# A hybrid decoder step: order of the opening, the new tokens' values, and the sums of the conv norm

## The chip, the core and the metric

The kernel runs on one core of a Trainium2 chip. The metric is the device time of one execution in microseconds, the median of three runs. Lower is better.

## What is computed

One layer of a decoder with two branches, on 512 prompt tokens and 32 new tokens (8 sequences of 4) together, 544 columns in all. Everything is f32.

```
h = RMSNorm_pre(x); z = h @ w_in        # columns: q | k | v | gate_attn | conv_a | conv_b | gate_conv
attention, 12 heads x 128: three dilated windows (128,1), (512,4), (2048,16), T5 bias, merged by softmax weight
conv, 512 channels: u = a * sigmoid(b); depthwise causal conv, width 31; LayerNorm over channels; swish; pointwise
mix = [att * silu(gate_attn), conv * silu(gate_conv)]
y = x + RMSNorm_post(mix @ w_out)
outputs: y for prompt and new tokens, new conv state, new k/v rows, the k/v cache shifted by 4 rows
```

The RMSNorm in front is not applied to x. Its per-token factor 1/rms (`R`) multiplies the products afterwards, since it is one number per token.

## The kernel before

**Projection.** `w_in` is cut into 60 blocks of 128 columns, `w_out` into four of 512. An f32 product is made as three products in a faster number format: x and the weights are split into a high and a low part (`xh`, `xl`, `wh`, `wl`), and TensorE adds xh·wh, xl·wh and xh·wl. One column block takes 96 products x 2 halves of 272 tokens. ScalarE casts `wh`, POOL subtracts to get `wl` (lines 819, 820); a piece of four 128x128 tiles is called a split.

**Opening.** `project_first` makes the first three column blocks side by side, by pieces of x as they land. Meanwhile `square` (line 283, ScalarE) sums the squares of five blocks of tokens (`mix` for four blocks of 128 tokens, `xt` for the 32 new ones), `token_rsqrt` makes the root on ScalarE (line 204) and a correction step on VectorE (lines 205 to 210), builds five diagonal matrices (line 212, `diagx`), and TensorE spreads them over all partitions by products with ones (`rbx`). ScalarE copies the two results to `R`. Only with `R` can the three column blocks be taken out of their banks.

**Side work.** After each half of a projection `tick` advances generators: attention of one head of the prompt, the new tokens' attention (`samples`, three groups of four heads), and the conv. In `v_phase` of the new tokens a unit is one sequence: eight pieces of four matmuls with a tile position each, seven over the cached rows (`kvf`, `kvm`) and one over the 32 new rows (`vtm`). The four sequences of a half stand side by side in one bank; `gather` copies it (`osb`, line 719), TensorE transposes it (`ot`), and VectorE writes the parts out.

**Conv norm.** `conv_ln` sums four channel blocks `cc` with ones on TensorE: `pm` for the mean, `pvar` over the squares `csq`, each in two halves of 272 tokens, f32 products that TensorE makes in several passes.

**Order.** All engines run their instructions in the order in which the program is written (`in_order`); a wait holds whatever is behind it on the same engine. All but one of the transfers are issued by SyncE in that order too. The copy of the cache (`bulk`) is spread over the run: at each tick it is issued up to START + PACE bytes per column that TensorE has been given (`pe`).

Of the kernel before, what the change touches and what calls it, by code (L numbers as in the profile page):

```python
# [42 lines left out]

UTK, UTV = 3.75, 3.3

START, PACE = 4_000_000, 166.3

NF = 3

# [36 lines left out]
def body(tc, xT, xtok, gpost, w_in, w_out, ckv, cconv, relb, vecs, pww, c_oht, c_ohr, c_lmr, c_tm, c_pick,  # L86
# [191 lines left out]
    def load_xtok(b):  # L278
        dma(xt_of(b), xtok[b * P:min(b * P + P, TOK)])

    def square(b):
        t_ = xt_of(b)
        nc.scalar.activation(t_, t_, AF.Square, accum_out=sumsq[:P if b < 4 else NS, b:b + 1])
# [182 lines left out]
    def conv_ln():  # L466
        cc = mixg[3]
        def load_pw(n):
            pw = apool.tile([P, 4, P], F32, tag="pw", name=f"pw{n}")
            dma(pw, pww[:, :, n * P:(n + 1) * P])  # L470
            return pw

        pw = load_pw(1)

        for hf in range(2):
            sl = slice(hf * HT, hf * HT + HT)
            pm = bank("z", f"pm{hf}")
            for ct in range(4):
                mm(pm[:, :HT], ones, cc[:, ct, sl], start=(ct == 0), stop=(ct == 3))
            for ct in range(4):  # L480
                nc.vector.scalar_tensor_tensor(cc[:, ct, sl], pm[:, :HT], -4.0, cc[:, ct, sl], op0=ALU.mult,
                                               op1=ALU.add)
            yield
        ri = apool.tile([P, TOK], F32, tag="q", name="cri")
        for hf in range(2):
            sl = slice(hf * HT, hf * HT + HT)
            csq = [apool.tile([P, 2, HT], F32, tag="up", name=f"csq{hf}_{i}", bufs=2) for i in range(2)]
            for ct in range(4):
                nc.scalar.activation(csq[ct // 2][:, ct % 2, :], cc[:, ct, sl], AF.Square)
            yield  # L490
            pv = bank("z", f"pvar{hf}")
            for ct in range(4):
                mm(pv[:, :HT], ones, csq[ct // 2][:, ct % 2, :], start=(ct == 0), stop=(ct == 3))
            vs = apool.tile([P, HT], F32, tag="ccv", name=f"vs{hf}")
            nc.scalar.copy(vs, pv[:, :HT])
            yield
            yield from rsqrt(ri[:, sl], vs, HT, 4.0, apool, tag="up")
            yield
        for ct in range(4):
            nc.vector.tensor_tensor(cc[:, ct, :], cc[:, ct, :], ri, op=ALU.mult)  # L500
            nc.scalar.activation(cc[:, ct, :], cc[:, ct, :], AF.Identity, bias=V(V_LNB, ct), scale=V(V_LNG, ct))
            th = apool.tile([P, TOK], F32, tag="up", name=f"cth{ct}", bufs=2)
            nc.scalar.activation(th, cc[:, ct, :], AF.Tanh, scale=0.5)
            nc.vector.scalar_tensor_tensor(cc[:, ct, :], th, 1.0, cc[:, ct, :], op0=ALU.add, op1=ALU.mult)
            yield

        res = [cc[:, 0, :]] + [apool.tile([P, TOK], F32, tag="up", name=f"pwo{i}", bufs=2) for i in range(2)]
        res.append(apool.tile([P, TOK], F32, tag="q", name="pwo2"))
        for n in (1, 2, 3, 0):
            for hf in range(2):  # L510
                sl = slice(hf * HT, hf * HT + HT)
                ps = bank("z", "pwp")
                for ct in range(4):
                    mm(ps[:, :HT], pw[:, ct, :], cc[:, ct, sl], start=(ct == 0), stop=(ct == 3))
                dst = res[n]
                nc.scalar.activation(dst[:, sl], ps[:, :HT], AF.Identity, bias=V(V_PWB, n), scale=0.5)
                yield
            if n:
                yield
                pw = load_pw((n + 1) % 4)  # L520
                yield
                yield
                yield
        for n in range(1, 4):
            nc.scalar.copy(cc[:, n, :], res[n])
        state["conv"] = True
        yield
# [182 lines left out]
    def v_phase(g):  # L710
# [5 lines left out]

        def gather(half, o):
            osb = sp.tile([P, 512], F32, tag="ktn", name=f"osb{g}_{half}")
            nc.scalar.copy(osb, o)
            yield  # L720
            ps = bank("q", f"ot{g}_{half}")
            for s in range(4):
                tr(ps[:, s * P:s * P + P], osb[:, s * P:s * P + P], ident)
            yield
            for s in range(4):
                b = half * 4 + s
                src = ps[:, s * P:s * P + P].rearrange("p (h r) -> p h r", h=G4)[:, :, NT * b:NT * b + NT]
                dst = mixg[g][:, :, SEQ + NT * b:SEQ + NT * b + NT]
                nc.vector.tensor_copy(dst, src)
            yield  # L730

        got = iter(())
        for half in range(2):
            o = bank("acc", f"o{g}_{half}")
            for s in range(4):
# [5 lines left out]
                far, mid = fars[u], mids[u]  # L741
                if b < 2:
                    tm_mm(g, "vk"[b])
                for j in range(8):
                    for hh in range(G4):
                        hs = slice(hh * NS, hh * NS + NS)
                        hc = slice(hh * P, hh * P + P)
                        if j < 7:
                            src = far[:, j, hc] if j < 3 else mid[:, j - 3, hc]
                            lt = pt[:, j, hs]  # L750
                        else:
                            src = smp[g]["vtm"][:, hc]
                            lt = pt[0:NS, 7, hs]
                        mm(o[hs, s * P:s * P + P], lt, src, start=(j == 0), stop=(j == 7),
                                         tile_position=(0, hh * NS))
                    if j == 2:
                        yield UTV / 2
                        if b < 2:
                            tm_take(g, "vk"[b], ("vnew", "qb")[b])
                        next(got, None)  # L760
                        load_mid(u + 1)
                if s < 3:
# [142 lines left out]
    def project_first(outs):  # L905
# [15 lines left out]
            nc.gpsimd.tensor_tensor(wl, raw, wh.bitcast(F32), op=ALU.subtract)  # L921
            return wh, wl

        def rows(c, ws, k0, k1):
            for n in range(NF):
                for k in range(4 * c + k0, 4 * c + k1):
                    wh, wl = [w[:, k % 4, :] for w in ws[n]]
                    for hf in range(2):
# [18 lines left out]
        for c in range(4):  # L947
            nxt = prepare(c + 1) if c < 3 else None
            if c == 2:
                square(0)  # L950
                square(1)
            if c == 3:
                for b in range(2, 5):
                    square(b)
                for a in range(3):
                    split(4 * NF + a)
            rows(c, ws, 0, 2)
            if c < 3:
                rows(c, ws, 2, 4)
            ws_, ws = ws, nxt  # L960
        make_R()
        rows(3, ws_, 2, 4)
        for n in range(NF):
            for hf in range(2):
                outs[n](hf, z[n])
# [22 lines left out]
        load_w(2 * n + 1)  # L988
        xrs[4 + n] = load_x(4 + n)
    xrs[7] = load_x(7)  # L990
    for b in (4, 0, 1, 2, 3):
        load_xtok(b)
    load_w(2 * NF)
    load_w(2 * NF + 1)
    load_tabs()
    first = []
# [319 lines left out]
```

## Time and profile before

| | |
|---|---|
| runs, median (lowest to highest) | 1162.44 us (1160.51 to 1165.23) |
| profiled execution, its time and its span | 1162.85 us, 1161.1 us |
| TensorE products busy | 1137.1 us, 98% of the span |
| VectorE, ScalarE, POOL busy | 681.5, 377.2, 402.0 us |
| moved by DMA | 401.92 MB, mean 346 GB/s |

A busy share says how long an engine had something in hand, not who sets the end. A TensorE that shows 98% and few waits is the engine whose queue makes the time, as long as its inputs come in time. Where another engine waits for TensorE, its waiting costs nothing.

### The profile page before, as it was taken

The numbers are of one execution on the slowest core, as the hardware profiler recorded it, in microseconds if no ns is written. First come the engines' busy times: TensorE is split into PE (matmuls) and PEld (weight loads), VectorE is DVE, ScalarE is ACT, GpSimd is POOL, SyncE is SP. The second block draws the span as 40 slices with busy tenths as digits, with TensorE's granted clock in tenths as the row PEclk, the third lists the DMA queues.
The fourth block names the chain that finished last, engine by engine and source line by source line (L and its number), as shares of the span: only waits on it lengthen the run. The fifth ranks groups of instructions, "written<-read, shape, count | busy, mean of one in ns | idle before, by whom it ended". The sixth has DMA issues, their size and how long they took to land.

```text
span 1161.1 us, 23634 instructions
## 1 busy us (share of the span) xinstructions
PE 1137.1 (98%) x9344; PEld 1031.5 (89%) x9344; DVE 681.5 (59%) x1997; ACT 377.2 (32%) x749; POOL 402.0 (35%) x353
## 2 busy tenths in 40 slices
PE   8899999999999999999999999999999999999996
PEld 8799999999999999999999998899999997776775
DVE  6306788899799988778324667882222246112126
ACT  6423333422123343331334334322222244223140
POOL 6143333334344332333233223243333464213130
PEclk9899999999999999999999999999999999999998
DMA  9989989899999999999998999799989979999956
GB/s 345 333 327 392 401 323 394 319 324 348 413 318 366 375 359 362 327 366 359 394 352 297 372 400 395 268 341 374 376 332 371 346 254 346 365 339 399 331 217 226
DMA packets 96082, 401.92 MB, mean 346 GB/s; under 512 B 14999, under 2 KB 17815, under 8 KB 89764
## 3 DMA queue, kind: packets, MB, share of 16 engines
q1 hardware_dynamic: 95828, 400.14, 93.8%
q8 instruction: 73, 1.20, 0.4%
q10 hardware_dynamic: 144, 0.28, 0.1%
q14 instruction: 37, 0.30, 0.1%
HBM read 388.65 MB, written 212.66 MB: 518 GB/s over the span
## 4 chain that ended last, share of the span: by engine, by line
PE 85%; DMA 6%; DVE 5%; ACT 1%; issue 1%; SPq 1%; DVEq 0%; ACTq 0%
PE z L107 56%; PE oz L107 13%; PE o L109 4%; DMA raw<-in_w_out_dram 3%; DVE qsc L638 2%; PE att L107 2%; PE s L107 2%; DMA mix<-in_xtok_dram 1%; PE pwp L107 1%; DMA raw<-in_w_in_dram 1%; PE t L113 1%; PE os L109 1%; DMA xr<-in_xT_dram 1%; PE qbp L113 1%; PE kt L113 1%
## 5 line engine op out<-in xcount | busy, mean ns | idle before, releaser
L107 PE MATMUL z<-xh,wh 128*128 128x272 f32 x1920 | 572.2, 298 | 1.6 <-ACT srow L668 0.8
L107 PE MATMUL z<-xh,wl 128*128 128x272 f32 x1920 | 553.6, 288 | 0.8 <-POOL wl L921 0.8
L107 PE MATMUL z<-xl,wh 128*128 128x272 f32 x1920 | 552.5, 288 | 0.9 <-DVE xl L265 0.9
L820 POOL TENSOR_TENSOR wl<-raw,wh 128x512 fp32r<-128x512 f32 x228 | 308.9, 1363 | 473.5 <-ACT wh L819 446.9
L107 PEld LDWEIGHTS z<-xh,wh 128*128 128x128 f32 x1920 | 362.4, 189 | 19.7 <-issue 13.7
L107 PEld LDWEIGHTS z<-xl,wh 128*128 128x128 f32 x1920 | 362.1, 189 | 3.1 <-DVE xl L265 1.1
L107 PEld LDWEIGHTS z<-xh,wl 128*128 128x128 f32 x1920 | 362.0, 189 | 1.0 <-POOL wl L921 1.0
L819 ACT CAST wh<-raw 128x512 fp32r<-128x512 f32 x228 | 139.1, 617 | 170.7 <-PE z L107 105.9
L344 DVE TENSOR_TENSOR t<-z,R 128x272 f32<-128x272 f32 x96 | 42.1, 438 | 187.5 <-PE z L107 179.9
L638 DVE SCALAR_TENSOR_TENSOR qsc<-kvf,qb 128x128 f32<-128x128 f32 x288 | 119.1, 414 | 8.8
L638 DVE SCALAR_TENSOR_TENSOR qsc<-kvm,qb 128x128 f32<-128x128 f32 x288 | 119.2, 414 | 8.6
L452 DVE SCALAR_TENSOR_TENSOR mix<-up,vec,mix 128x512 f32<-128x512 f32 x120 | 103.7, 864 | 0.0
L107 PE MATMUL oz<-owh,mh 128*128 128x512 f32 x256 | 102.7, 401 | 0.0
L107 PE MATMUL oz<-owh,ml 128*128 128x512 f32 x256 | 100.9, 394 | 0.1
L107 PE MATMUL oz<-owl,mh 128*128 128x512 f32 x256 | 100.9, 394 | 0.0
L854 POOL TENSOR_TENSOR owl<-raw,owh 128x512 fp32r<-128x512 f32 x43 | 58.7, 1381 | 108.7 <-ACT owh L853 108.2
L107 PEld LDWEIGHTS oz<-owh,mh 128*128 128x128 f32 x256 | 48.1, 188 | 22.9 <-issue 6.7
L854 DVE TENSOR_TENSOR owl<-raw,owh 128x512 fp32r<-128x512 f32 x21 | 22.6, 1077 | 74.6 <-ACT owh L853 74.6
L853 ACT CAST owh<-raw 128x512 fp32r<-128x512 f32 x64 | 37.4, 618 | 83.3 <-DMA raw<-in_w_out_dram 74.8
L454 DVE SCALAR_TENSOR_TENSOR mix<-us,vec,mix 128x32 f32<-128x32 f32 x120 | 59.7, 498 | 0.0
L107 PEld LDWEIGHTS oz<-owl,mh 128*128 128x128 f32 x256 | 48.3, 189 | 11.4
L107 PEld LDWEIGHTS oz<-owh,ml 128*128 128x128 f32 x256 | 48.1, 188 | 11.1 <-DVE ml L797 0.5
(184 smaller groups left out, 1008.2 us busy)
## 6 DMA issues: line engine op xcount, KB each, us to landing
out_dram<-in_ckv_dram SPq DMA_DIRECT2D x168, 1152.0 KB, 11.9
raw<-in_w_in_dram SPq DMA_DIRECT2D x119, 512.0 KB, 10.6
kvm<-in_ckv_dram SPq DMA_DIRECT2D x48, 1024.0 KB, 10.3
kvf<-in_ckv_dram SPq DMA_DIRECT2D x144, 256.0 KB, 8.6
raw<-in_w_out_dram SPq DMA_DIRECT2D x32, 512.0 KB, 8.6
out_dram<-t SPq DMA_DIRECT2D x24, 256.0 KB, 7.8
mix<-in_xtok_dram SPq DMA_DIRECT2D x4, 1024.0 KB, 13.4
xt<-in_xtok_dram SPq DMA_DIRECT2D x8, 512.0 KB, 4.8
```

Source lines behind the costliest of these rows:

```text
L107: nc.tensor.matmul(out, lhsT, rhs, start=start, stop=stop)
L109: nc.tensor.matmul(out, lhsT, rhs, start=start, stop=stop, tile_position=tile_position)
L113: nc.tensor.transpose(out, in_, eye)
L344: nc.vector.tensor_tensor(dst[:, sl], z[hf][:, :HT], R[:, sl], op=ALU.mult)
L452: nc.vector.scalar_tensor_tensor(cc[:, ct, :SEQ], up[:, j:j + SEQ], wj, cc[:, ct, :SEQ], op0=ALU.mult, op1=ALU.add)
L454: nc.vector.scalar_tensor_tensor(cs, us[:, :, j:j + NT], wj, cs, op0=ALU.mult, op1=ALU.add)
L638: nc.vector.scalar_tensor_tensor(scr, src[:, hh * P:hh * P + P], SCALE, qb[:, hh * P:hh * P + P], op0=ALU.mult, op1=ALU.mult, accum_out=sd ...
L819: nc.scalar.copy(wh, raw)
L820: nc.gpsimd.tensor_tensor(wl, raw, wh.bitcast(F32), op=ALU.subtract)
L853: nc.scalar.copy(wh, raw)
L854: (nc.vector if j % 3 == 2 else nc.gpsimd).tensor_tensor(wl, raw, wh.bitcast(F32), op=ALU.subtract)
```

## The change

It does five things. In the opening the new tokens' squares come first and one cast of the next block between the others; the two other casts go behind the root; the transfer of the next weights goes ahead of the last two token blocks; and the products that spread the scale stand behind two of the three column blocks' last products instead of ahead of all. In `v_phase` the products over the new rows are made once per group, for all eight sequences at once, into a tile `ov`, which is added when a half is taken out, on VectorE instead of ScalarE's copy. In `conv_ln` the four channel blocks are added on POOL first (`total`), and TensorE makes one product per sum. PACE goes from 166.3 to 167.9.

```diff
-START, PACE = 4_000_000, 166.3
+START, PACE = 4_000_000, 167.9
...
+        def total(parts, name):
+            a = apool.tile([P, NB * (NT + CW - 1)], F32, tag="us", name=f"ca{name}", bufs=2)[:, :HT]
+            b = apool.tile([P, NB * (NT + CW - 1)], F32, tag="us", name=f"cb{name}", bufs=2)[:, :HT]
+            nc.gpsimd.tensor_tensor(a, parts[0], parts[1], op=ALU.add)
+            nc.gpsimd.tensor_tensor(b, parts[2], parts[3], op=ALU.add)
+            nc.gpsimd.tensor_tensor(a, a, b, op=ALU.add)
+            return a
...
-            for ct in range(4):
-                mm(pm[:, :HT], ones, cc[:, ct, sl], start=(ct == 0), stop=(ct == 3))
+            mm(pm[:, :HT], ones, total([cc[:, ct, sl] for ct in range(4)], f"m{hf}"), start=True, stop=True)
...
-            nc.scalar.copy(osb, o)
+            nc.vector.tensor_tensor(osb.rearrange("p (s c) -> p s c", s=4), o.rearrange("p (s c) -> p s c", s=4),
+                                    ov[:, None, :].to_broadcast([P, 4, P]), op=ALU.add)
...
+        def new_mm():
+            ps = bank("q", f"ov{g}")
+            for hh in range(G4):
+                hs = slice(hh * NS, hh * NS + NS)
+                mm(ps[hs, 0:P], pt[0:NS, 7, hs], smp[g]["vtm"][:, hh * P:hh * P + P], start=True, stop=True,
+                   tile_position=(0, hh * NS))
+            return ps
...
-                for j in range(8):
+                if b == 3:
+                    new = new_mm()
+                for j in range(7):
...
+                        if b == 3:
+                            nc.scalar.copy(ov, new[:, 0:P])
...
             if c == 2:
-                square(0)
-                square(1)
+                for b in (4, 0, 1):
+                    square(b)
+                split(4 * NF)
             if c == 3:
-                for b in range(2, 5):
-                    square(b)
-                for a in range(3):
-                    split(4 * NF + a)
+                square(2)
+                square(3)
...
+        rows(3, ws_, 2, 4, (0, 1))
         make_R()
-        rows(3, ws_, 2, 4)
+        for a in range(1, 3):
+            split(4 * NF + a)
+        rows(3, ws_, 2, 4, (2,))
...
-    for b in (4, 0, 1, 2, 3):
+    for b in (4, 0, 1):
         load_xtok(b)
     load_w(2 * NF)
+    for b in (2, 3):
+        load_xtok(b)
```

ScalarE in the opening, from the last pieces of x to the copies of the scale. `mix_98`, `mix_99`, `mix_100`, `mix_97` are the four blocks of 128 tokens, `xt` the 32 new ones, `wh` the casts of the fourth column block, `rx` the root. Before, and then now:

```order
32 L283 ACTIVATE mix_98,sumsq<-mix_98 128x2048
33 L283 ACTIVATE mix_99,sumsq<-mix_99 128x2048
34 L283 ACTIVATE mix_100,sumsq<-mix_100 128x2048
35 L283 ACTIVATE mix_97,sumsq<-mix_97 128x2048
36 L283 ACTIVATE xt_107,sumsq<-xt_107 32x2048
37 L819 CAST wh_509<-raw_152 128x512
38 L819 CAST wh_513<-raw_152 128x512
39 L819 CAST wh_519<-raw_154 128x512
40 L204 ACTIVATE rx<-sumsq,epsc 128x5
41 L324 COPY R<-rbx_575 128x272
```

```order
32 L283 ACTIVATE xt_107,sumsq<-xt_107 32x2048
33 L283 ACTIVATE mix_98,sumsq<-mix_98 128x2048
34 L283 ACTIVATE mix_99,sumsq<-mix_99 128x2048
35 L838 CAST wh_435<-raw_150 128x512
36 L283 ACTIVATE mix_100,sumsq<-mix_100 128x2048
37 L283 ACTIVATE mix_97,sumsq<-mix_97 128x2048
38 L204 ACTIVATE rx<-sumsq,epsc 128x5
39 L324 COPY R<-rbx_589 128x272
40 L324 COPY R<-rbx_593 128x272
41 L838 CAST wh_599<-raw_150 128x512
42 L838 CAST wh_605<-raw_154 128x512
```

The small square has moved to the front, one cast between the squares, two casts behind the root and behind the copies of `R`. On TensorE, around the products that spread the scale, now: `z_1_171` is the second of the three column blocks of the opening, `z_0_172` the third.

```order
276 L107 MATMUL z_1_171<-xl_427,wh_414 128x272
277 L107 MATMUL z_1_171<-xh_426,wl_415 128x272
278 L107 MATMUL rbx_589<-diagx,ones 128x128 x2
279 L107 MATMUL rbx_589<-diagx,ones 128x16
280 L107 MATMUL rbx_593<-diagx,ones 128x112
281 L107 MATMUL rbx_593<-diagx,ones 128x128
282 L107 MATMUL rbx_593<-diagx,ones 128x32
283 L107 MATMUL z_0_172<-xh_422,wh_418 128x272
```

Twenty-four products that stood behind the spread now stand ahead of it, twelve stay behind. On POOL, around the conv norm, now: `cam`, `cbm` and `cav`, `cbv` are the partial sums for mean and variance, `wl` the weight subtractions.

```order
189 L839 TENSOR_TENSOR wl_6886<-raw_6649,wh_6885 128x512
190 L477 TENSOR_TENSOR cam_6917<-mix_100 128x272
191 L478 TENSOR_TENSOR cbm_6918<-mix_100 128x272
192 L479 TENSOR_TENSOR cam_6917<-cam_6917,cbm_6918 128x272
193 L839 TENSOR_TENSOR wl_6933<-raw_6740,wh_6932 128x512
194 L477 TENSOR_TENSOR cam_6983<-mix_100 128x272
195 L478 TENSOR_TENSOR cbm_6984<-mix_100 128x272
196 L479 TENSOR_TENSOR cam_6983<-cam_6983,cbm_6984 128x272
197 L839 TENSOR_TENSOR wl_6994<-raw_6740,wh_6993 128x512
198 L839 TENSOR_TENSOR wl_7050<-raw_6832,wh_7049 128x512
199 L477 TENSOR_TENSOR cav_7078<-csq_0_7040 128x272
```

Before, only the weight subtractions stood in this place; now four times three additions stand between them.

## Rows read from the trace of the kernel before

**Rows 1.** The page, part 1: busy us (share of the span), instructions.

```profile
PE 1137.1 (98%) x9344; PEld 1031.5 (89%) x9344; DVE 681.5 (59%) x1997; ACT 377.2 (32%) x749; POOL 402.0 (35%) x353
```

**Rows 2.** TensorE's waits, all of them: us in total, times, longest.

```profile
PE rbx L107 <- DVE diagx L212: 4.9, 1, 4.9
PE s L107 <- DVE pr L369: 1.9, 2, 1.7
```

**Rows 3.** Stretches: length, busy by engine, then granted clock, DMA share, GB/s.

```profile
0.00:1100.00 1100.00, 1085.14 (x9112) 992.31 (x9113) 651.80 (x1928) 361.86 (x715) 391.05 (x346) 1.00 0.96 353
...
40.00:60.00 20.00, 14.05 (x80) 12.46 (x79) 6.86 (x21) 3.43 (x9) 3.82 (x4) 0.83 0.89 303
...
100.00:200.00 100.00, 99.17 (x794) 92.86 (x793) 86.41 (x372) 37.25 (x83) 34.26 (x36) 1.00 0.98 381
```

**Rows 4.** TensorE in order of time, 40 to 53: start, length, idle before.

```profile
40.01 0.29 PE L107 MATMUL z<-xh,wl 128*128 128x272 f32 x1
45.24 2.74 PE L107 MATMUL rbx<-diagx,ones 128*128 128x128 f32 x12 [4.94 <-DVE diagx L212]
47.79 0.57 PE L107 MATMUL z<-xh,wh 128*128 128x272 f32 x1
48.16 0.43 PE L107 MATMUL z<-xl,wh 128*128 128x272 f32 x1
...
52.20 0.29 PE L107 MATMUL z<-xl,wh 128*128 128x272 f32 x1
```

**Rows 5.** ScalarE in order of time, 31 to 42.

```profile
31.22 1.92 ACT L283 ACTIVATE mix<-mix 128x2048 f32<-128x2048 f32 x1 [0.50 <-DMA mix<-in_xtok_dram]
...
36.19 1.92 ACT L283 ACTIVATE mix<-mix 128x2048 f32<-128x2048 f32 x1 [0.49 <-DMA mix<-in_xtok_dram]
...
38.10 1.90 ACT L283 ACTIVATE xt<-xt 32x2048 f32<-32x2048 f32 x1
...
39.99 1.64 ACT L819 CAST wh<-raw 128x512 fp32r<-128x512 f32 x3
41.54 0.29 ACT L204 ACTIVATE rx<-sumsq,epsc 128x5 f32<-128x5 f32 x1
```

**Rows 6.** VectorE in order of time, 43 to 45.

```profile
43.20 1.19 DVE L208 TENSOR_TENSOR wx<-wx,vx 128x5 f32<-128x5 f32 x1
44.42 0.17 DVE L209 TENSOR_SCALAR wx<-wx 128x5 f32<-128x5 f32 x1
```

**Rows 7.** POOL in order of time, 40 to 45.

```profile
40.67 3.70 POOL L820 TENSOR_TENSOR wl<-raw,wh 128x512 fp32r<-128x512 f32 x3 [10.74 <-DMA ohr<-in_c_ohr_dram]
```

**Rows 8.** One unit's new tokens' products by time; then their group by line.

```profile
805.62 0.42 PE L109 MATMUL o<-vtm,spt 32*32 32x128 f32 x8
...
805.97 0.39 PE L107 MATMUL z<-xh,wh 128*128 128x272 f32 x1
...
L109 PE MATMUL o<-vtm,spt 32*32 32x128 f32 x192 | 10.1, 280 | 0.0
```

**Rows 9.** A tap on VectorE and the transposes, group 0, second half.

```profile
343.48 0.74 DVE L452 SCALAR_TENSOR_TENSOR mix<-up,vec,mix 128x512 f32<-128x512 f32 x1
...
348.52 0.60 PE L113 MATMUL ot<-ident,osb 128*128 128x128 f32 x4
```

**Rows 10.** The chain that ended last, 552 to 571: start, length, what.

```profile
552.98 1.83 PE pm L107 x8
...
568.22 1.83 PE pvar L107 x8
```

**Rows 11.** Around the conv norm by time: VectorE's last tap, POOL's subtraction.

```profile
547.70 0.24 DVE L454 SCALAR_TENSOR_TENSOR mix<-us,vec,mix 128x32 f32<-128x32 f32 x1
...
563.37 1.28 POOL L820 TENSOR_TENSOR wl<-raw,wh 128x512 fp32r<-128x512 f32 x1 [1.67 <-ACT wh L819]
```

**Rows 12.** Busy by engine: six stretches of 240 to 360 summed, and 800 to 900.

```profile
sum 120.00, PE 120.00 PEld 112.60 DVE 111.95 ACT 27.19 POOL 47.72; mean PE 20.00 PEld 18.77 DVE 18.66 ACT 4.53 POOL 7.95
...
800.00:900.00 100.00, 100.00 (x1135) 93.06 (x1134) 21.07 (x29) 20.38 (x35) 38.25 (x28) 1.00 0.96 358
```

More of the change, by code (lines that the diff above doesn't have):

```diff
@@ L491, in conv_ln @@
             pv = bank("z", f"pvar{hf}")
-            for ct in range(4):
-                mm(pv[:, :HT], ones, csq[ct // 2][:, ct % 2, :], start=(ct == 0), stop=(ct == 3))
+            mm(pv[:, :HT], ones, total([csq[ct // 2][:, ct % 2, :] for ct in range(4)], f"v{hf}"), start=True,
+               stop=True)
             vs = apool.tile([P, HT], F32, tag="ccv", name=f"vs{hf}")
@@ L732, in v_phase @@
         got = iter(())
+        ov = sp.tile([P, P], F32, tag="ov", name=f"ov{g}")
+        def new_mm():
[5 more added lines that the diff above has]
+            return ps
         for half in range(2):
@@ L747, in v_phase @@
                         hc = slice(hh * P, hh * P + P)
[L748 to L754, printed above, removed]
+                        src = far[:, j, hc] if j < 3 else mid[:, j - 3, hc]
+                        mm(o[hs, s * P:s * P + P], pt[:, j, hs], src, start=(j == 0), stop=(j == 6),
                                          tile_position=(0, hh * NS))
@@ L922, in split_first, with rows @@
             return wh, wl
-        def rows(c, ws, k0, k1):
-            for n in range(NF):
+        def rows(c, ws, k0, k1, ns=range(NF)):
+            for n in ns:
                 for k in range(4 * c + k0, 4 * c + k1):
```

## The prediction

> **What bounds the kernel now.** I read the page's busy shares first: TensorE is busy 98% of the span [rows 1]. A busy matmul engine may still be waiting inside its pipeline, so the second view was TensorE's own waits. In 1161.1 us they hold one large entry, 4.9 us in front of the products that spread the token scale; the next is 1.9 us in two waits [rows 2]. So TensorE sets the time nearly everywhere, and what is taken from its queue should come off the end, unless a wait that its work covers today becomes visible. The third view was the stretches, for the transfers: they are busy 0.96 of the first 1100 us at 353 GB/s [rows 3]. That is close to full, so it is weighed below. The profiled execution took 1162.85 us, 1.75 us beyond its span; the median of the runs is 1162.44, 0.4 us lower. I make the sum against 1162.85.
>
> **Part 1, the opening.** TensorE starts its last product at 40.01 and idles until 45.24; that is the 4.94 us wait for the diagonals [rows 4]. Then the clock is low: the granted clock of 40 to 60 is 0.83 on average [rows 3], and products that start every 0.125 us elsewhere are 0.23 us apart, which is 272 columns at 1.2 GHz instead of 2.4 (48.16 to 52.20 holds 18 steps, 0.224 each, the last a short one). The wait is made by ScalarE [rows 5]: its squarings of 128 tokens wait for token rows (the second ends its wait at 31.22, the fourth at 36.19, so one 1 MB block lands every 2.5 us), then the 32 sample rows' square runs (38.10 to 40.08), then three weight casts (39.99 to 41.63), and only then the root at 41.54. The root's chain on VectorE ends in the diagonals for which TensorE waits; a 128x5 product in it takes 1.19 us [rows 6] while POOL subtracts weights from 40.67 to 44.37 [rows 7].
>
> The change puts the sample rows' square first, one cast into a gap, and two casts with their POOL subtractions behind the root. A weight load of half a block's size now goes ahead of the last two blocks, so these land half of 2.5 us later: the last near 37.45 and not 36.19. A square step takes 2.0 us, and the first of them is over 0.50 us before 31.22, so ScalarE is free for them from 28.7. The ends are then 30.7, 32.7, 34.7 (the block of 31.22 is there), cast 35.3, then 37.3, then the last from 37.45 to 39.45; the root follows at 39.5, two us earlier. At the old length of its chain (41.54 to 45.24, 3.7 us) the diagonals are ready at 43.2. With POOL silent meanwhile, that product should fall towards the 0.17 us of the 128x5 step behind it [rows 6], and it is 42.2. TensorE meanwhile has 24 more products in front of the spread: 40.14 + 24 x 0.125 = 43.14. So no wait in either case, by 0 to 0.9 us, and so no low clock. The six spreading products hold 544 columns, twice the 272 that cost 1.83/4 = 0.46 us in the group that is priced in part 3: 0.92. Then 12 products, 1.5 us: this part ends at 45.6. Before, the same products start at 47.79, the twentieth at 52.20 and sixteen more follow: 54.2 + 0.125 = 54.33. Gain 8.7 us. What is next late: the scale's copies on ScalarE and the two casts and subtractions now behind them. With 0.55 us a cast and 1.23 a subtraction (a third of the groups in [rows 5, 7]) and 0.4 a copy of 272 columns, estimated from the cast of 512, the second weight piece is there at about 46.4, and TensorE asks for it after 12 products of the fourth column block, at 47.1. I take 8.5. If the last block lands 3 us later than I work out, a wait of some 3 us returns with part of the low clock: gain 4.
>
> **Part 2, the new tokens' values.** Each of 24 units (3 groups, 8 samples) ends with four matmuls with 32 rows. The row of one unit: the new tokens' burst starts at 805.62 behind the cached pieces, the next projection at 805.97 [rows 8]. The step from a burst of 128 rows to the next kind of product remains, so 0.35 us goes per unit: 24 x 0.35 = 8.4. They are now done once per group: 3 x 0.35 = 1.05 comes back. Net 7.35. The row gives each of these records 280 ns, eight to a unit [rows 8]. The Trainium skill (TensorE: Matmul & The Clock Gate, Part 3, Measured speedup vs the span model) says that packed tiles cost the duration of one matmul and about 4 ns for each further tile; that would be 0.28 + 7 x 0.004 = 0.31 a unit, 6.5 net as an estimate, 0.9 less than by the row, and the sum goes by the row.
>
> The new values are added on VectorE, in place of six ScalarE copies of 128x512: six additions that read PSUM, 0.7 us each by VectorE's 128x512 taps (0.74 in [rows 9]), 4.1 us. Six times TensorE's transposes wait for them. The tightest place is the second half of group 0: VectorE reaches the place at 343.48, so the sum is there at 344.2, and the transposes start at 348.52 [rows 9]. 4 us remain, or 1.5 us when TensorE comes 2.45 us earlier (8 x 0.35 - 0.35). Cost on the path: 0, up to 2 us.
>
> **Part 3, the conv norm.** Each of four sums over channels is four f32 products of 272 columns, 1.83 us [rows 10]; one remains, so 3/4 goes: 4 x 1.37 = 5.5 us. POOL gets twelve additions of 128x272. The trace has none; its 128x512 subtraction takes 1.27, so in proportion 0.68, and I take 0.75 for a fixed part, 2.25 for three. They must fit between their input and TensorE's arrival. First sum: the last tap ends at 547.94 on VectorE and TensorE comes at 552.98 [rows 10, 11]; 2.8 us spare. The tightest is the first variance: POOL's subtraction ahead of it ends at 564.65, the sums at 566.9, TensorE was there at 568.22 [rows 10, 11]; 1.3 us spare. So 0. Were an addition as long as the 128x512 subtraction, 1.27, the three would take 3.8: a wait of 2.5 us here and 1.0 at the first sum, with the low clock behind it some 5 us for all; that is the upper bound.
>
> **Pace.** The bulk copy is issued by TensorE columns. Fewer columns at 167.9 and not 166.3 bytes each send about the same bytes at the same stage: 12 x 272 x 4 + 84 x 128 = 23.8 thousand columns go, about 1% of them, and the rate rises by 1%. Cost 0; it is the rate per us that rises, by 1.9%.
>
> **Sum.** 8.5 + 7.35 + 5.5 = 21.35; 1162.85 - 21.35 = 1141.5.
>
> **The rivals.**
> *VectorE holds group 0.* From 240 to 360 VectorE is busy 111.95 of 120 us in the records [rows 12]. If it is the true bound there, TensorE's 2.45 us are not given, and the two additions (1.4) come on top: 3.9 us back, 1145.4. For it: that share. Against: TensorE shows no wait there above the 1.9 us of [rows 2], and VectorE stands 4 us ahead at the place of [rows 9].
>
> *The transfers take it back.* Arriving 21 us earlier asks for 360 GB/s where 353 were moved [rows 3]. If 353 is the limit, half of the gain or more goes: about 1152. Against: the stretch from 100 to 200 moves 381 GB/s at 0.98 [rows 3], and a full queue that is still in time shows no limit yet.
>
> *The opening keeps its wait,* because the reordered loads land 3 us later than worked out: gain 4 there, 1146. For it: between the old chain and TensorE's arrival stand 0.0 us. Against: the 3.7 us hold the 1.19 us product, and the root is reckoned from landings that the rows show.
>
> *The additions stop TensorE* (slower). One mechanism: VectorE's six additions come late and the transposes behind them wait, and after each wait the clock is low, as after the diagonals, for 18 products at 0.1 us more, 1.8 us. With a wait w the six cost 6 x (w + 1.8). At w = 1.8 nothing is left of 21.35; over 2.7 us the kernel is slower by more than 5.8 us: about 1169. For it: VectorE is full at two of the six places. Against: it is busy 21.07 of 100 us from 800 to 900, where two others lie [rows 12], and the copy that the addition replaces waits for the same products of TensorE.
>
> *The change does less than it says*: the f32 sums might not cost by count. The row of 1.83 us for four products and the columns agree, so I give this nothing of its own.
>
> **How the numbers follow.** Forecast 1141.5, with 1138.5 to 1144.5 for the sizes: 0.62. VectorE in group 0, the opening or a late POOL sum, alone or two of them, 1144.5 to 1150: 0.22. Transfers, 1150 to 1156: 0.07. Within 0.5% of 1162.44 (5.8 us, about what a measurement of this kernel can tell from no change): 0.05. Slower: 0.02. Below 1138.5: 0.02. Range 1138.5 to 1150. Faster by over 0.5%: 0.93.
>
> **What would show it.** In the profile after: no wait of TensorE at the spreading products, clock 1.0 from 40 to 60, the first column block behind them done some 8.5 us earlier; the new tokens' products three times and not 24, and the way from the first to the last unit of a group shorter by 2.45 us; sums of mean and variance 0.46 us long without a wait for POOL. I am wrong if TensorE's waits name POOL's sums, VectorE's additions or a transfer with more than 3 us together, or if its busy time falls by 13 us and the span by much less.

## The result, and the profile after

The changed kernel takes 1149.24 us in the median (1148.74 to 1151.47, four runs); the kernel before took 1161.78 beside it. The ratio is 0.9885 with a 95% interval of 0.9869 to 0.9902: faster by 12.5 us. The forecast was 1141.5; the time lies 7.7 us above it, inside the range, near its upper end. The profiled execution took 1151.47 us with a span of 1149.7, so that by profiles the gain is 11.4 us.

The page of the kernel after, part 1, answers to [rows 1]:

```profile
PE 1128.1 (98%) x9152; PEld 1025.6 (89%) x9152; DVE 685.6 (60%) x2003; ACT 374.4 (33%) x746; POOL 411.5 (36%) x365
```

TensorE's waits, the largest of them (us in total, times, longest), answer to [rows 2]:

```profile
PE os L109 <- DMA raw<-in_w_out_dram: 5.5, 2, 4.0
PE s L107 <- DVE pr L369: 1.9, 2, 1.7
...
PE tb L107 <- ACT tabs L309: 0.7, 1, 0.7
...
PE rb L107 <- ACT tabs L309: 0.3, 1, 0.3
```

The 4.9 us in front of `rbx` are gone, as meant. Now a wait for weights of `w_out` heads the list, 5.5 us at the products `os` that project the 32 sample rows. It is not new: in the same view of the kernel before it stands third, and [rows 2] stops one line ahead of it:

```profile
PE os L109 <- DMA raw<-in_w_out_dram: 1.7, 1, 1.7
```

Nothing in the list names the sums on GpSimd (POOL) or VectorE's additions.

Where the gain lies is read from the start of the same product in both traces. The lead of the kernel after over the one before, in us, is worked out from these starts. An output product is one of the 768 products `oz` of the output stage, in order; column blocks are counted from 0, so 3 is the first behind the opening's three:

| place | lead | what lies between |
|---|---|---|
| column block 3, behind the spread | 7.55 | the opening |
| column blocks 4 to 15 | 5.99 | the position tables (-1.56) |
| column blocks 22 to 32 | 8.37 | values of group 0 (+2.38) |
| column blocks 39 to 49 | 16.27 | conv norm and values of group 1 (+7.9) |
| column block 59, end of projections | 18.74 | values of group 2 (+2.47) |
| output product 192 | 19.09 | |
| output product 240 | 11.61 | **-7.48** |
| output product 432 | 13.92 | +2.31, the kernel before waits here for w_out (1.7 us) |
| output product 624, and the end | 11.37 | **-2.55** |

So 18.7 us had been won when the projections ended, and 7.4 us on balance were lost again in the output stage, the last 200 us. TensorE in order of time at the larger loss (start, length, idle time before, with what ended it):

```profile
984.41 0.40 PE L107 MATMUL oz<-owl,mh 128*128 128x512 f32 x1
984.74 1.05 PE L109 MATMUL os<-raw,smix 128*32 128x512 f32 x4
989.79 1.92 PE L109 MATMUL os<-raw,smix 128*32 128x512 f32 x4 [4.00 <-DMA raw<-in_w_out_dram]
991.65 0.80 PE L107 MATMUL oz<-owh,mh 128*128 128x512 f32 x1
...
993.09 0.63 PE L107 MATMUL oz<-owh,mh 128*128 128x512 f32 x1
993.52 0.63 PE L107 MATMUL oz<-owh,ml 128*128 128x512 f32 x1
...
995.18 0.40 PE L107 MATMUL oz<-owl,mh 128*128 128x512 f32 x1
995.41 0.40 PE L107 MATMUL oz<-owh,mh 128*128 128x512 f32 x1
```

TensorE stands still for 4.00 us, and then its products start 0.43 us apart instead of 0.23 until 995.2: 512 columns at 1.2 GHz, not 2.4. The wait, the 0.87 us by which the second `os` group is longer than the first, and some eight products at 0.2 us more (1.6) make 6.5 of the 7.5 us. The stretches show the low clock (0.83 from 985 to 1005); the transfers are busy 0.97 of the first 1100 us and 0.88 of this stretch (columns as in [rows 3]):

```profile
0.00:1100.00 1100.00, 1087.46 (x8972) 994.64 (x8973) 659.52 (x1938) 363.81 (x722) 406.04 (x362) 0.99 0.97 356
40.00:60.00 20.00, 18.99 (x125) 16.58 (x125) 4.61 (x20) 5.05 (x11) 4.16 (x5) 0.91 1.02 351
100.00:200.00 100.00, 99.17 (x796) 92.96 (x795) 83.40 (x357) 36.63 (x83) 32.96 (x35) 1.00 1.01 394
985.00:1005.00 20.00, 15.99 (x61) 10.06 (x58) 3.47 (x3) 5.70 (x10) 9.30 (x7) 0.83 0.88 349
```

Why the weights came late is read from SyncE, which issues all transfers but one, in order. Its waits from 940 to 990, and what it issued from 946 on:

```profile
SPq L98 <- PE os L109: 17.6, 3, 12.6
SPq L98 <- DMA out_dram<-in_ckv_dram: 13.9, 4, 4.0
```

```profile
946.01 6.86 SPq L98 DMA_DIRECT2D out_dram<-in_ckv_dram  x6
956.95 0.33 SPq L98 DMA_DIRECT2D raw<-in_w_out_dram  x1
957.99 4.57 SPq L98 DMA_DIRECT2D out_dram<-in_ckv_dram  x2
966.09 13.36 SPq L98 DMA_DIRECT2D raw<-in_w_out_dram  x2
```

Eight copies of the cache (`out_dram<-in_ckv_dram`, 1152 KB each by the page) stand around two loads of w_out. In the built program each transfer waits for one of eight semaphores, used in turn, so it is issued only when the transfer eight places ahead has landed; in order, as SyncE issues them:

```
out_dram<-in_ckv_dram 32x9216 [waits DMAHW2_49]
out_dram<-in_ckv_dram 32x9216 [waits DMAHW3_49]
raw_12513<-in_w_out_dram 128x1024 [waits DVE_49,DMAHW4_49,PE_49,Pool_49]
out_dram<-in_ckv_dram 32x9216 [waits DMAHW5_49]
out_dram<-in_ckv_dram 32x9216 [waits DMAHW6_49]
raw_12537<-in_w_out_dram 128x1024 [waits DVE_49,DMAHW7_49,PE_49,Pool_49]
```

So a load can have seven transfers ahead of it. The second of these two has six copies and the first load: 7.6 MB, some 22 us at the 350 GB/s of the page (an estimate). SyncE itself is held for 13.9 us until earlier copies have landed, and the load that TensorE will need at 985.8 is issued at 966.09, when the copy eight places ahead of it, issued at 946.56, has landed (966.01); in the trace the load lands at 989.75, 23.7 us later. The list of issues gives 15.0 us as the median from issue to landing of the w_out loads, 8.6 before; the trace tells the landing of only 9 of the 32 here and of 13 before, so these medians are rough, and the longest are 23.7 to 27.1 us here and 23.4 to 23.7 before:

```profile
out_dram<-in_ckv_dram SPq DMA_DIRECT2D x168, 1152.0 KB, 11.7
raw<-in_w_in_dram SPq DMA_DIRECT2D x119, 512.0 KB, 10.8
...
raw<-in_w_out_dram SPq DMA_DIRECT2D x32, 512.0 KB, 15.0
```

The three parts themselves. The opening, on ScalarE, VectorE and TensorE (answers to [rows 4 to 6]):

```profile
37.63 1.92 ACT L283 ACTIVATE mix<-mix 128x2048 f32<-128x2048 f32 x1
...
39.67 0.30 ACT L204 ACTIVATE rx<-sumsq,epsc 128x5 f32<-128x5 f32 x1
```

```profile
40.43 0.17 DVE L208 TENSOR_TENSOR wx<-wx,vx 128x5 f32<-128x5 f32 x1
...
41.11 1.07 DVE L212 TENSOR_SCALAR diagx<-ident,rx 128x128 f32<-128x128 f32 x5
```

```profile
43.81 0.29 PE L107 MATMUL z<-xh,wl 128*128 128x272 f32 x1
43.94 1.42 PE L107 MATMUL rbx<-diagx,ones 128*128 128x128 f32 x12
45.19 0.37 PE L107 MATMUL z<-xh,wh 128*128 128x272 f32 x1
```

The root stands at 39.67 and the diagonals are done at 42.18, 1.8 us before TensorE asks. The new tokens' values and the conv norm by groups (count, busy us, mean ns, idle before; answer to [rows 8, 10]):

```profile
L727 DVE TENSOR_TENSOR osb<-o,ov 128x512 f32<-128x512 f32 x6 | 4.1, 688 | 6.6 <-PE o L109 6.6
...
L477 POOL TENSOR_TENSOR cam<-mix 128x272 f32<-128x272 f32 x2 | 1.6, 776 | 0.0
...
L109 PE MATMUL ov<-vtm,spt 32*32 32x128 f32 x24 | 1.3, 280 | 0.0
```

The new tokens' products are 24 records and not 192. VectorE's additions wait for TensorE, 6.6 us in all, in groups 1 and 2, and TensorE shows no wait for them.

### The profile page after: what moved, and what is told of

The parts are those of the page before. It is cut to its first block, busy times and chain, and to the rows that moved or that the text cites. A ratio compares the mean times of both kernels' runs of the same rounds, so it can differ in the third digit from the quotient of the medians.

```text
span 1149.7 us, 23274 instructions
## 1 busy us (share of the span) xinstructions
PE 1128.1 (98%) x9152; PEld 1025.6 (89%) x9152; DVE 685.6 (60%) x2003; ACT 374.4 (33%) x746; POOL 411.5 (36%) x365
## 4 chain that ended last, share of the span: by engine, by line
PE 83%; DMA 10%; DVE 4%; POOL 1%; ACT 1%; issue 1%; SPq 0%; DVEq 0%; POOLq 0%; ACTq 0%
PE z L107 57%; PE oz L107 10%; DMA raw<-in_w_out_dram 5%; PE o L109 4%; DMA out_dram<-in_ckv_dram 2%; DVE qsc L646 2%; PE s L107 2%; PE att L107 2%; DMA raw<-in_w_in_dram 1%; PE pwp L107 1%; PE t L113 1%; PE os L109 1%; PE qbp L113 1%; PE kt L113 1%; PE sn L109 1%
## 5 line engine op out<-in xcount | busy, mean ns | idle before, releaser
L344 DVE TENSOR_TENSOR t<-z,R 128x272 f32<-128x272 f32 x96 | 42.0, 438 | 175.5 <-PE z L107 167.9
L452 DVE SCALAR_TENSOR_TENSOR mix<-up,vec,mix 128x512 f32<-128x512 f32 x120 | 108.4, 903 | 0.0
L873 DVE TENSOR_TENSOR owl<-raw,owh 128x512 fp32r<-128x512 f32 x21 | 23.7, 1127 | 80.8 <-ACT owh L872 80.8
L454 DVE SCALAR_TENSOR_TENSOR mix<-us,vec,mix 128x32 f32<-128x32 f32 x120 | 56.7, 473 | 0.0
```

Source lines behind the costliest of these rows:

```text
L344: nc.vector.tensor_tensor(dst[:, sl], z[hf][:, :HT], R[:, sl], op=ALU.mult)
L452: nc.vector.scalar_tensor_tensor(cc[:, ct, :SEQ], up[:, j:j + SEQ], wj, cc[:, ct, :SEQ], op0=ALU.mult, op1=ALU.add)
L454: nc.vector.scalar_tensor_tensor(cs, us[:, :, j:j + NT], wj, cs, op0=ALU.mult, op1=ALU.add)
L873: (nc.vector if j % 3 == 2 else nc.gpsimd).tensor_tensor(wl, raw, wh.bitcast(F32), op=ALU.subtract)
```

## The experiments

Two theories stood against each other for the 7.4 us. **T1**: the output stage is short of transfer time; TensorE gets there some 19 us earlier, finds w_out loads behind cache copies, and pays a wait and low clock. **T2**: the stage is slow for another reason (the weight loads themselves, the clock), or, as T2b, the number that the change set to 167.9 bytes per column is at fault by itself. A part that does not give what the sum says was the third possibility. Each set of runs has its own runs of the kernel before beside it, 1162.6 to 1163.1 us in the median.

### The copies of the output stage

**Left out altogether:**

```diff
-                    tick()
+                    now[0] += 1
+                    flush_late(now[0])
...
-                if 2 in bs:
-                    bulk(1 << 60)
```

> The changed kernel, but the copies of the cache from device memory to device memory that belong to the output stage are not issued (the rest of the cache in the output stays unwritten); the weight loads of w_out and everything else stay. Theory T1, the transfers take back the gain: between the units oz192 and oz240 the lead over the kernel before fell from 19.1 to 11.6 us, because the w_out load issued at 966.1 landed only at 989.8, behind copies. Without the copies that wait of TensorE (4.0 us) and the low clock behind it go, and the 7.5 us come back: about 1141 to 1142 us in the median. Theory T2, the weight load itself or TensorE's clock sets this place whatever the copies do: 1148 to 1150, with a wait of about 4 us left.

Measured: 1140.12 us (1138.97 to 1140.47), ratio 0.9799 [0.9786, 0.9813]. TensorE's list of waits has no entry for w_out; from issue to landing its loads take 4.2 us in the median (of the 8 whose landing the trace tells):

```profile
raw<-in_w_out_dram SPq DMA_DIRECT2D x32, 512.0 KB, 4.2
```

The lead over the kernel after rises by 7.47 us between output products 192 and 240 and by 2.5 at product 624, the two places of the losses. T1 holds for the stage: copies are the cause. Without them TensorE waits for no w_out load. (A further 1.84 us of this run's lead is there before the stage begins; it comes from the opening.)

**Given out more slowly in this stage alone**, 155, 161 and 144 bytes per TensorE column instead of 167.9:

```diff
-        bulk(START + PACE * pe[0])
+        bulk(START + PACE * pe[0] - (PACE - 155.0) * (pe[0] - out0[0] if out0 else 0))
...
+    out0.append(pe[0])
```

> The changed kernel; in the output stage alone the cache copies are given out at 155 bytes per TensorE column instead of 167.9, and what is left goes out behind the last column. Theory T1: part of the wait of 4.0 us and of the low clock goes, 1143 to 1148, as long as the copies left for the end land before the last output. Theory T2 (the copies in this stage are not the cause): 1148 to 1150 or, if the copies at the end come late, above 1151.

> As the run with 155 bytes per column in the output stage, with 161: half of the step from 167.9. Theory T1 (the rate of the copies in this stage decides, by degrees): between the 1141.3 of 155 and the 1146.5 to 1149.2 of 167.9, so 1141 to 1146, with a wait for w_out of 0 to 2 us. Rival (155 helped because the last copies shifted, not by the rate): 1146 to 1150 with a wait above 2 us.

> As the run with 155 bytes per column in the output stage, with 144. Theory T1: the wait is gone, 1141 to 1145, unless the copies left for the end set the end, then up to 1150 with the last transfer as the end of the chain. Theory T2: 1148 to 1150 with the wait left.

Measured: 1141.33 us at 155 (1141.28 to 1142.51; ratio 0.9814 [0.98, 0.9827]), 1141.23 at 161 (1140.64 to 1142.09; 0.9808 [0.9794, 0.9821]), 1148.54 at 144 (1146.67 to 1149.54; 0.9871 [0.9857, 0.9885]). With all copies still made, a rate 4% lower in the last fifth of the kernel brings the whole forecast: both beat the changed kernel by 5 to 8 us. At 161 TensorE at the same place, and SyncE's waits from 940 to 990:

```profile
983.88 0.40 PE L107 MATMUL oz<-owl,mh 128*128 128x512 f32 x1
984.21 1.87 PE L109 MATMUL os<-raw,smix 128*32 128x512 f32 x8
986.00 0.50 PE L107 MATMUL oz<-owh,mh 128*128 128x512 f32 x1
```

```profile
SPq L98 <- PE os L109: 25.2, 4, 15.2
SPq L98 <- DVE owl L874: 7.5, 5, 2.4
SPq L98 <- DMA out_dram<-in_ckv_dram: 6.2, 2, 4.3
```

All eight products of the sample rows run in one piece; SyncE waits 6.2 us for copies instead of 13.9, and the two loads in question are issued at 952.51 and 960.63 instead of 956.95 and 966.09, 5.5 us earlier for the second while TensorE comes 0.5 us earlier. It needs little: between the two loads stands one copy and not two. The step from 161 to 155 brings nothing more, against "by degrees" in the expectation.

At 144 TensorE has no wait for w_out either, and its last product ends at 1129.59, eleven us before the changed kernel's 1140.62. But the copies left over then stand in front of the last token rows; of the longest pieces of the chain that ended last, these are the end:

```profile
1083.95 5.79 PE oz L107 x24
1090.80 21.64 DMA xt<-in_xtok_dram
1121.88 8.05 DMA xt<-in_xtok_dram
```

and the end comes 18.2 us behind the last product instead of 9.1. The gain is given back at the tail: the copies have a place between too early and too late.

### The number of bytes per column

**166.3 in the changed kernel**, as before the change, in the whole kernel:

```diff
-START, PACE = 4_000_000, 167.9
+START, PACE = 4_000_000, 166.3
```

> The changed kernel with the number of bytes per TensorE column set back from 167.9 to the 166.3 of the kernel before, nothing else. Theory T2b, the new number moved the copies onto the w_out loads: about 1142, the wait of 4 us gone. Theory T1, the output stage is short of transfer time because TensorE reaches it 18.7 us earlier with the same bytes to move: 1147 to 1151, with a wait of some us in the same stage.

**167.9 in the kernel before**, nothing else:

```diff
-START, PACE = 4_000_000, 166.3
+START, PACE = 4_000_000, 167.9
```

> The kernel before with the one number of the change alone: 167.9 bytes per TensorE column instead of 166.3. Theory T1 (the number hurts only where TensorE reaches the output stage early): the kernel before still has slack there, 1161 to 1164. Theory T2b (the number itself costs the 5 us by which 166.3 was faster in the changed kernel): 1166 to 1169.

**The changed kernel once more**, as it is:

> The changed kernel once more, as it is, beside the same runs of the kernel before, so that 1149.2 stands against the 1144.0 and 1141.3 of the kernels with another number from this chip. Both theories: 1148 to 1151, again with a wait of TensorE for w_out of 2 us or more and a low clock behind it.

Measured: 1144.03 us (1142.55 to 1146.04; ratio 0.9837 [0.9823, 0.9851]) for 166.3 in the changed kernel; 1162.80 for 167.9 in the kernel before, against 1162.59 (0.9996 [0.9987, 1.0005], eleven runs); 1146.47 (1144.99 to 1147.72; 0.9864 [0.9848, 0.9879]) for the changed kernel again, on another chip than the 166.3, below the 1148 that was expected. T2b falls for the kernel before: the number costs it nothing. In the changed kernel neither expectation was met, and the intervals of 0.9837 and 0.9864 just touch, so the number's own share is not settled; it lies between 0 and some 5 us. With 166.3 the waits for w_out are shorter but still there:

```profile
PE os L109 <- DMA raw<-in_w_out_dram: 1.1, 2, 0.8
```

The repetition is worth most for its profile. In this execution the lead at column block 3 is 8.68 us, at column block 59 20.72, and in front of output product 240 20.82; then it falls to 17.37 with a wait of 2.49 us for w_out, and to 17.01 at the end:

```profile
983.01 1.05 PE L109 MATMUL os<-raw,smix 128*32 128x512 f32 x4
986.55 1.05 PE L109 MATMUL os<-raw,smix 128*32 128x512 f32 x4 [2.49 <-DMA raw<-in_w_out_dram]
```

So the same program loses 3.8 us in this stage in one execution and 7.7 in another, by how late the load comes and whether the clock falls behind it: the granted clock from 985 to 1005 is 1.00 here, and 0.83 in the first profile. The expected wait of 2 us or more is there, the low clock is not.

### Each part alone, on the kernel before, with 166.3

**The opening:** squares, root, casts, the place of the spreading products and the order of the loads (cut).

```diff
             if c == 2:
-                square(0)
-                square(1)
+                for b in (4, 0, 1):
+                    square(b)
+                split(4 * NF)
             if c == 3:
-                for b in range(2, 5):
-                    square(b)
...
+                square(2)
+                square(3)
...
+        rows(3, ws_, 2, 4, (0, 1))
         make_R()
...
+        rows(3, ws_, 2, 4, (2,))
...
-    for b in (4, 0, 1, 2, 3):
+    for b in (4, 0, 1):
         load_xtok(b)
     load_w(2 * NF)
+    for b in (2, 3):
+        load_xtok(b)
```

> The kernel before with the new order of the opening alone (squares, root, casts, spreading products in the middle of the last chunk), 166.3 bytes per column. By the prediction's sum the wait of 4.94 us goes and the first column block behind the spreading products begins 8.5 us earlier; by the profiles of the changed kernel that is 7.5 to 8.8 us at that block and 6.0 to 8.7 us behind the tables, by whether TensorE's clock falls there. Theory T1 (the transfers of the output stage take back a lead when it grows): this lead alone is less than half of the full one, so most of it lives: 1154 to 1157 us. Rival (the opening gives its lead back later to the weight loads): 1159 to 1163.

**The values:** the products of the new tokens once per group.

```diff
-                for j in range(8):
+                if b == 3:
+                    new = new_mm()
+                for j in range(7):
```

> The kernel before with the products of the new tokens' values once per group alone. By the prediction's sum 24 small products of 0.35 us less 3 of them: 7.35 us, 1155 to 1156, in three steps of 2.45 us, each inside a group. Rival (six VectorE additions in the place of ScalarE copies hold TensorE): a gain under 3 us, 1160 or more. Theory T1 alone takes nothing from it or little, as the lead at the output stage is 7.35 us.

**The conv norm:** additions on GpSimd.

```diff
-            for ct in range(4):
-                mm(pm[:, :HT], ones, cc[:, ct, sl], start=(ct == 0), stop=(ct == 3))
+            mm(pm[:, :HT], ones, total([cc[:, ct, sl] for ct in range(4)], f"m{hf}"), start=True, stop=True)
```

> The kernel before with the additions of the conv norm on GpSimd alone. By the prediction's sum 4 times 1.37 = 5.5 us: 1157 to 1158. Rival (the additions on GpSimd arrive late and TensorE waits for them): 1161 to 1169, with waits of the mean and variance products on GpSimd.

**The place of the spreading products alone**, with ScalarE's order as before:

```diff
+        rows(3, ws_, 2, 4, (0, 1))
...
-        rows(3, ws_, 2, 4)
+        rows(3, ws_, 2, 4, (2,))
```

> The kernel before with the spreading products and what needs them moved behind 24 more products of the last opening chunk, but ScalarE's order of squares, casts and root as before. By the prediction's steps TensorE comes 24 x 0.12 = 2.9 us later to these products and the diagonals are ready as late as before (45.24), so the wait falls from 4.94 to about 2 us: a gain of 3 us, 1159 to 1161. Rival (the place of the products is all, the order on ScalarE nothing): wait gone, 1155 to 1157 as with the whole opening. Rival (a wait of 2 us still lowers the clock): 1161 to 1163.

| run | time, us | ratio [interval] | lead where the part ends | at the end |
|---|---|---|---|---|
| opening | 1156.33 (1152.78 to 1158.94) | 0.9941 [0.9926, 0.9956] | 8.48 at block 3, 5.70 from block 6 | 6.13 |
| values | 1157.39 (1155.56 to 1161.57) | 0.9954 [0.9939, 0.9970] | 2.38 + 2.46 + 2.51 in the three groups | 6.53 |
| conv norm | 1157.98 (1156.78 to 1158.51) | 0.9954 [0.9943, 0.9966] | 5.50 between blocks 32 and 39 | 5.86 |
| place of the spread | 1158.88 (1156.69 to 1160.62) | 0.9967 [0.9954, 0.9980] | 3.88 at block 3, 3.52 from block 4 | 5.06 |

The leads are against the one profile of the kernel before; the profile of the values alone stands 0.65 us ahead and that of the conv norm 0.5 us ahead before their part begins. On TensorE values and conv norm are worth what the sum said, to a tenth. In time the values give 5.6 us and not 7.35, short of the 1155 to 1156 expected: of their lead of 8.02 us at the end of the projections 3.5 go in the output stage, 2.4 of them between output products 192 and 240 again, with a wait of 1.38 us for w_out, and 2.1 come back where the kernel before has its own wait. So a lead of 8 us is enough for the loss to begin, against the "nothing from it or little" of the expectation. The opening brings 8.48 where its wait was, and gives 2.8 back over the next three blocks. The place of the products alone leaves a wait, 3.25 us and not 2, since the diagonals are ready at 46.35 here:

```profile
42.80 0.29 PE L107 MATMUL z<-xh,wl 128*128 128x272 f32 x1
46.35 1.52 PE L107 MATMUL rbx<-diagx,ones 128*128 128x128 f32 x12 [3.25 <-DVE diagx L212]
47.71 0.45 PE L107 MATMUL z<-xh,wh 128*128 128x272 f32 x1
47.95 0.43 PE L107 MATMUL z<-xl,wh 128*128 128x272 f32 x1
```

with products 0.23 us apart behind it: a wait of 3 us still lowers the clock. The place alone does not bring the whole opening; the order on ScalarE alone was not run.

### The position tables later

On the kernel with 155 in the output stage, the tables three ticks later:

```diff
-                add(make_tabs(), 11, 0)
+                add(make_tabs(), 14, 0)
```

> The changed kernel with 155 bytes per column in the output stage and, new, the position tables three ticks later in the column block (14 instead of 11), so that their small products don't meet ScalarE's table work. Theory: in the profiles TensorE's clock falls behind two short waits at these products (0.66 and 0.34 us) in some executions and costs up to 2 us; with the tables later the waits shrink and the time is 0.5 to 2 us below that of 155 alone: 1139.5 to 1141. Rival (each product of the tables waits for ScalarE's step on the one before it, wherever they stand, or the rotation that needs the tables comes late): 1141 to 1145.

Measured: 1141.21 us (1139.10 to 1143.93; ratio 0.9821 [0.9807, 0.9835]), no difference from 1141.33. In its profile the lead at column block 4 is 10.07 instead of 6.74 us, but by block 6 it is 8.32: part goes to the next weights. The profiled execution is 2.25 us faster than that of 155, the median is not; whether the place of the tables matters stays open.

## Why the prediction was right, and where it failed

**The range held, but not for its reasons.** The time lies under 1150. The prediction put 1144.5 to 1150 down to VectorE in group 0, the opening or a late POOL sum. In the first profile the opening lost 2.5 us of its 8.5 and the other two nothing; most of what is missing went to the transfers, for which 1150 to 1156 was named at a chance of 0.07. That this loss still left the time inside the range was luck. By the prediction's own sign of being wrong, waits for a transfer of more than 3 us together, it was wrong on this: 5.5 us, and 3.6 in the repetition.

**Part 2, the new tokens' values, 7.35: right.** In the run of this part alone the three groups give 2.38, 2.46 and 2.51, together 7.35; in the whole change group 0 gives 2.38 too. The step to the next kind of product that the row shows, 0.35 us a unit, is what was paid. By the Trainium skill (TensorE: Matmul & The Clock Gate, Part 3, Measured speedup vs the span model), with about 4 ns for each further packed tile, it would have been 6.5 us, an estimate; the 7.35 measured decide. The six additions cost TensorE nothing, 0.69 us each where 0.7 was taken. The rival *VectorE holds group 0* is out, since group 0 gave its 2.4 us; but VectorE did not wait there for TensorE. Its two additions start 4.1 and 3.1 us after the products that they need, and the second ends 2.2 us before TensorE's transposes start, where 1.5 was reckoned.

**Part 3, the conv norm, 5.5: right.** 5.50 alone. POOL's additions took 0.77 us (0.75 taken), and TensorE has no wait for them: the first variance's sum ends at 554.86 and its product starts at 555.94, 1.1 us later, where 1.3 was worked out:

```profile
553.22 0.78 POOL L478 TENSOR_TENSOR cbv<-csq 128x272 f32<-128x272 f32 x1
554.08 0.78 POOL L479 TENSOR_TENSOR cav<-cav,cbv 128x272 f32<-128x272 f32 x1
...
555.94 0.62 PE L107 MATMUL pvar<-cav,ones 128*128 128x272 f32 x2
```

**Part 1, the opening, 8.5: mechanism right, term too large for what lives.** The wait is gone, root and diagonals stood within 0.2 us of the sum (39.67 and 42.18), VectorE's 128x5 product fell from 1.19 us to 0.17. In seven of the nine profiles with the whole opening the lead at column block 3 is 8.3 to 8.8 us; in the first profile of the kernel after it is 7.55, and there the clock was low earlier, 0.90 from 10 to 20. What the sum lacks comes behind it. The tables' small products wait 0.66 and 0.34 us for ScalarE, and in that profile TensorE then runs at 1.2 GHz until 56.4 (granted clock 0.83 from 50 to 60; 1.00 in the repetition); in other profiles, as those of the repetition and of the opening alone, TensorE waits for the next split weights instead, by up to 0.8 us. With the tables in their place that leaves 5.7 to 7.9 us of 8.5 at column block 7. I had put the second weight piece 0.7 us ahead of TensorE and the tables nowhere. "Clock 1.0 from 40 to 60" was wrong for this profile: 0.91.

**The transfers: the step that failed.** The sum says under *Pace* "Cost 0; it is the rate per us that rises, by 1.9%", and gives the rival *The transfers take it back* 0.07, because 381 GB/s were moved elsewhere and "a full queue that is still in time shows no limit yet". The run without copies in the output stage, 1140.12, and those with slower copies, 1141.2 to 1141.3, show this rival at work, and in one stage only. I had weighed the queue as a rate over 1100 us. What counts is one load's slack at one place: before, the w_out load issued at 979.84 landed at 1003.57, after 23.7 us as well, and the first product that reads it started at 1004.28: a slack of 0.7 us. In the kernel after TensorE came 19.1 us earlier to this place, but the load was issued only 13.8 us earlier, at 966.09, and had the same 23.7 us in front of it: the 5.3 us between are the slack of 0.7 and a delay of 4.6, of which 4.0 show as idle time. The rows of before that tell this, single loads with issue, landing and first use in the output stage, I had not read, and the 1.7 us for w_out in the list of waits, which said that a load there was late already, I had left out of [rows 2]. The price named for the rival (half of the gain, 1152) was about right for the first runs, its place and chance were not.

The load and its products in the kernel before (the fifth of the eight, at 1004.28, is the first to read it):

```profile
979.84 0.33 SPq L98 DMA_DIRECT2D raw<-in_w_out_dram  x1
...
1003.82 1.06 PE L109 MATMUL os<-raw,smix 128*32 128x512 f32 x8
```

**The number 167.9** costs nothing in the kernel before, as the sum had it; in the changed kernel it was not shown to be free.

**Sum.** At the end of the projections 18.7 to 20.7 us of the forecast 21.35 are there; the output stage takes 7.7 and 3.8 in the two profiles of the changed kernel. The kernels with slower copies reach the forecast time, but not by its sum alone: at 155 the lead at output product 0 is 19.49 and 21.5 at the end, because the kernel before itself loses some 2 us in its output stage, at its own wait for w_out (output products 384 to 432 take it 16.3 us, 13.6 with 155). The last condition on record, busy time down by 13 and the span by less, does not describe what came: TensorE's busy time fell by 9.0 in the first profile, where the clock was low in places, and by 13.7 in the repetition, and its span by 11.4 and 17.1.

## What to carry to other kernels

When a kernel's engine and its transfers are both nearly full, time won on the engine is kept only where loads have slack: before forecasting, follow single loads of the later stages from issue to landing to first use, above all where copies without a deadline share their queue. Such copies want a rate for each stage, low enough that no load stands behind a burst and high enough that none are left for the tail. A short wait is to be priced with the clock behind it, and the profile of one execution shows only one of its outcomes.

## What the runs showed of the hardware

A wait of 4.00 us at the w_out products cost 7.5 us, one of 2.49 us in another execution of the same program 3.45: behind the first the granted clock was 0.83 from 985 to 1005, behind the second 1.00. With the clock at 1.00 the loss is about 1 us more than the idle time shown: 3.45 for 2.49, 2.42 for 1.38 (values alone), 1.79 for 0.84 (166.3). Two waits of 0.66 and 0.34 us at the tables were followed by 1.2 GHz in one execution and by 2.4 in the other.

A w_out load of 512 KB takes 3.6 to 5.2 us from issue to landing between 930 and 1100 us where no copies are about. Behind copies the loads whose landing the trace tells take up to 23.7 us in the kernel before, 27.1 in the kernel after and 27.9 with 161 bytes per column, and 23.7 in the one that TensorE waited for: what is in flight ahead sets it, hardly the load's own size. With 161 the two loads in question are issued 4.4 and 5.5 us earlier; the first takes 27.9 us, and the landing of the second the trace does not tell.
